# Moving small work between engines in the attention stage of a two-block transformer kernel: one head of a pair scaled on ScalarE, narrow top-k rounds paired, a log polynomial and six logarithms rearranged

## The chip, the cores and the metric

The kernel runs on one core of one Trainium2 chip. The metric is device time in microseconds (us), the median over repeated executions. All arithmetic of the reference is float32. The engines are named as in the profile: PE (TensorE, matrix products; PEld is its weight load), DVE (VectorE), ACT (ScalarE), POOL (GpSimd) and SP (SyncE, which issues the DMA transfers).

## The reference, cut to what matters

Two residual blocks of two layers each, on 256 tokens of width 1024. The change touches only the second block: its three attention branches.

```python
def _layer(x, positions, g_mix, w_in, b_forget, w_branch, w_out, g_mlp, w_up, w_down):
    h = _rmsnorm(x, g_mix)
    (qa, ka, va, qb, kb, vb, fl, qc, kc, vc, qi, ki, wi, gl) = split(h @ w_in)
    br_a = _stick_breaking_attention(qa, ka, va)              # 8 heads of 64
    log_f = log_sigmoid(fl + b_forget)                        # 256 x 8
    br_b = _forgetting_attention(qb, kb, vb, log_f)           # bias: cumsum of log_f
    br_c = _indexed_sparse_attention(rope(qc), rope(kc), vc, rope(qi), rope(ki), wi, top_k)
    gates = sigmoid(gl)
    x = x + (sum over branches of gates * (br @ w_branch)) @ w_out
    return x + square(relu(rmsnorm(x) @ w_up)) @ w_down

# stick breaking, per query row:
#   w = exp(log_sigmoid(z) + (sum of log_sigmoid(-z) over later keys)), strict causal mask
# forgetting: softmax(z + c[t] - c[s]) with c = cumsum(log_f)
# indexed sparse: score = sum_i w_i relu(q_i . k); keep the top_k = 64 keys; softmax over them
```

## The kernel before

A float32 product is made on PE as three products of rounded parts (`mm3`: high by high, high by low, low by high). So every float32 tile that PE multiplies is first *split*: a high part by a copy on ACT (L265 for weights, L297 for activations) and a low part by a subtraction on DVE (L267 and L298, for some weights POOL). Weights come from HBM in units of 512 KB, issued on SP some units ahead, and are split about three units before PE uses them. PE therefore carries a nearly unbroken stream of projections.

The attention branches are written as Python generators (`spawn`), each of which hands over at every `yield`. While the projections of the layer are written out, a tick after a group of matmuls lets two tasks of the deque take one step each. So a `yield` is not a wait on the chip: it sets how far apart two steps of a branch stand in the instruction streams of the engines, and what of the other branches and of the projections stands between them. Each engine runs its own stream in order; a wait for another engine's result holds up all that stands behind it on that engine. `wait(n)` is n yields, that is n turns.

The steps of one layer that the change touches:

- `neg_log1p_exp` (L887 to L906) computes log sigmoid for the forgetting branch's 256 x 8 gate inputs (tile 128x16): s = e/(2+e) with e = exp(-|x|), q = s*s, and a polynomial in q by Horner's rule, nine turns of a product (L901) and an addition of a constant (L902), each on the result of the one before. After it the result is multiplied by s (L904) and put together (L906). `lf_task` then copies it (L1624), and PE sums it up over the tokens by a product with a triangle of ones (L1630, L1631). The first block calls the same function.
- `dsa_task` (L1640 on), the sparse branch: index scores, then for each of the two blocks of 128 query rows eight rounds of `max` (L1667, the eight largest of a row) and `match_replace` (L1668), 64 keys in all. Rows of block 0 have 128 keys (narrow), rows of block 1 have 256. Then four pairs of heads, each with two calls of `attend`.
- `fox_task`, the forgetting branch: four pairs with two calls of `attend` each. It begins after `lf_task`.
- `attend` (L1462 on): scores on PE; on DVE scores plus mask or bias with the row maximum (L1471); the exponential with the row sum on ACT; the reciprocal of two sums (L1478) and the scaling of both heads on DVE (L1480); transposes on PE (L1485); the transposed heads copied out of PSUM, head 0 on DVE, head 1 on ACT (L1489). There are 32 calls in all: two branches, four pairs, two blocks, two layers.
- `sb_task`, the stick-breaking branch, six tiles of 128x512: log(1+exp) by ACT's Exp (L1773) and Ln (L1780), masks (DVE L1788, POOL L1790), then a split whose high part (L1796) and low part (L1798) are both made on POOL; PE sums the parts (L1802, L1803).

The order of the six splits is tiles 4, 5, 0, 1, 2, 3, and that of the six logarithms 0 to 5, with a turn after every second one. `after` lets a task begin when others are done. The order of instructions on each engine follows from these turns alone; there is no table of priorities.

Of the kernel before, what the change touches and what calls it, by code (L numbers as in the profile page):

```python
# [11 lines left out]
F32 = mybir.dt.float32  # L12
# [3 lines left out]
AF = mybir.ActivationFunctionType  # L16
ALU = mybir.AluOpType
# [83 lines left out]
def two_block_kernel(ctx: ExitStack, tc: tile.TileContext, A, out):  # L101
    nc = tc.nc
    pe, dve, act, pool, sp = nc.tensor, nc.vector, nc.scalar, nc.gpsimd, nc.sync

    def wait(n):
        for _ in range(n):
            yield
# [8 lines left out]
    tp = ctx.enter_context(tc.tile_pool(name="tp", bufs=2))  # L116
# [767 lines left out]
        for l in range(DEPTH):  # L884
            dve.tensor_scalar(nlam[:, l:l + 1], lam[:, l:l + 1], LAM_INIT[l], -1.0, op0=ALU.add, op1=ALU.mult)

    def neg_log1p_exp(o, x, n, pool_):  # L887

        e = T(pool_, [P, n], "lp_e")
        a = T(pool_, [P, n], "lp_a")  # L890
        s = T(pool_, [P, n], "lp_s")
        q = T(pool_, [P, n], "lp_q")
        dve.scalar_tensor_tensor(a, x, -1.0, x, op0=ALU.mult, op1=ALU.max)
        act.activation(e, a, AF.Exp, scale=-1.0)
        dve.tensor_scalar(a, e, 2.0, None, op0=ALU.add)
        dve.reciprocal(a, a)
        dve.tensor_tensor(s, e, a, op=ALU.mult)
        dve.tensor_tensor(q, s, s, op=ALU.mult)
        dve.memset(e, 1.0 / 19)
        for k in range(8, -1, -1):  # L900
            dve.tensor_tensor(e, e, q, op=ALU.mult)  # L901
            dve.tensor_scalar(e, e, 1.0 / (2 * k + 1), None, op0=ALU.add)  # L902
            yield
        dve.tensor_tensor(e, e, s, op=ALU.mult)  # L904
        dve.tensor_scalar(a, x, 0.0, None, op0=ALU.min)
        dve.scalar_tensor_tensor(o, e, -2.0, a, op0=ALU.mult, op1=ALU.add)  # L906
# [535 lines left out]
    xb = [xb[0], xb[1]]  # L1442


    SHE, SLE = pool, pool
    tri = cp.tile([P, 2, P], F32R, name="tri")
    dve.tensor_copy(tri[:, 0], C("negge"))
    dve.tensor_copy(tri[:, 1], C("negone"))
# [13 lines left out]
    def attend(tb, pair, scores, bias, v, pT):  # L1462

        S_ = P * (tb + 1)
        ps = sm_bank()[:, :2 * S_].rearrange("p (j s) -> p j s", j=2)
        scores(ps, tb, pair, S_)
        yield
        z = t2([P, 2, 256])[:, :, :S_]
        st = small(8)
        for j in range(2):  # L1470
            dve.tensor_tensor_reduce(z[:, j], ps[:, j], bias(tb, 2 * pair + j), 1.0, -3.0e38,  # L1471
                                     op0=ALU.add, op1=ALU.max, accum_out=st[:, j:j + 1])
        dve.tensor_scalar(st[:, 2:4], st[:, 0:2], -1.0, None, op0=ALU.mult)
        yield
        for j in range(2):
            act.activation(z[:, j], z[:, j], AF.Exp, bias=st[:, 2 + j:3 + j], accum_out=st[:, 4 + j:5 + j])
        yield
        dve.reciprocal(st[:, 6:8], st[:, 4:6])  # L1478
        for j in range(2):
            dve.tensor_scalar(z[:, j], z[:, j], st[:, 6 + j:7 + j], None, op0=ALU.mult)  # L1480
        yield
        pt = sm_bank()[:, :2 * S_].rearrange("p (j s) -> p j s", j=2)
        for j in range(2):
            for sb in range(tb + 1):
                pe.transpose(pt[:, j, sb * P:(sb + 1) * P], z[:, j, sb * P:(sb + 1) * P], ident)  # L1485
        yield
        for j in range(2):
            o = pT[j][:, 0:P] if tb == 0 else pT[j][:, P:3 * P]
            (act.copy if j else dve.tensor_copy)(o, pt[:, j])  # L1489
# [11 lines left out]
    def block2_layer(l, hT, rms):  # L1501
# [85 lines left out]
        lfx = T(tp, [P, 2, 8], "lfx")  # L1587
        lf = T(tp, [P, 2, 8], "lf")
# [27 lines left out]
        def lf_task():  # L1616
            yield from after([t_ki])

            f2 = lambda t: t.rearrange("p a b -> p (a b)")
            yield from neg_log1p_exp(f2(lf), f2(lfx), 16, tp)  # L1620
            lf2 = T(tp, [P, 2, 40], "lf2")
            pool.memset(lf2, 0.0)
            for k in range(2):
                dve.tensor_copy(lf2[:, :, 32 * k:32 * k + 8], lf)  # L1624

            nlo = cst[:, COFF["negle"][0]:COFF["negle"][0] + 256]
            for _ in range(LFY):
                yield
            ps = sm_bank()[0:40, 0:256]
            pe.matmul(ps, lf2[:, 0], nlo, start=True, stop=False)  # L1630
            pe.matmul(ps[:, P:], lf2[:, 1], nlo[:, :P], start=False, stop=True)  # L1631
            yield
            par = C("par")
            for k in range(2):
                act.activation(cs[0:40, k], ps, AF.Copy, scale=par[0:40, k:k + 1])
            for k in range(2):
                dve.scalar_tensor_tensor(cs[32:40, k], ps[32:40], par[32:40, k:k + 1], cs[32:40, k].bitcast(F32),
                                         op0=ALU.mult, op1=ALU.subtract)
# [4 lines left out]
        def dsa_task():  # L1643
            yield from after(t_c + [t_ki])
            for tb in range(2):
                S_ = P * (tb + 1)
                wv = small(4)
                dve.tensor_scalar(wv, tail[tb][:, 96:100], 0.5, None, op0=ALU.mult)
                scv = t2([P, 256])[:, :S_]
                for p_ in range(2):  # L1650
                    ps = sm_bank()[:, :2 * S_].rearrange("p (j s) -> p j s", j=2)
                    mm3(ps, *(t[:, p_, tb * P:(tb + 1) * P] for t in qiT), kiD[:, 0, :, :S_], kiD[:, 1, :, :S_],
                        start=True, stop=True)
                    yield
                    r = t2([P, 2, 256])[:, :, :S_]
                    act.activation(r, ps, AF.Relu, scale=0.125)
                    for j in range(2):
                        i = 2 * p_ + j
                        if i == 0:
                            dve.tensor_scalar(scv, r[:, j], wv[:, 0:1], None, op0=ALU.mult)  # L1660
                        else:
                            dve.scalar_tensor_tensor(scv, r[:, j], wv[:, i:i + 1], scv, op0=ALU.mult, op1=ALU.add)
                    yield
                dve.tensor_tensor(scv[:, tb * P:], scv[:, tb * P:], causal, op=ALU.add)
                m8 = small(8)
                for it in range(8):
                    dve.max(m8, scv)  # L1667
                    dve.match_replace(scv, m8, scv, GONE)  # L1668
                    yield
                M = Ms[tb]  # L1670
                dve.tensor_scalar(M, scv, -2.0e38, -NEG, op0=ALU.is_lt, op1=ALU.mult)
                dve.tensor_scalar(M, M, NEG, None, op0=ALU.add)
                dve.tensor_tensor(M[:, tb * P:], M[:, tb * P:], causal, op=ALU.add)
                yield

            def scores(ps, tb, pair, S_):
                qh, ql = (t[:, pair % 2, tb * P:(tb + 1) * P] for t in qcT[pair // 2])
                kh, kl = (t[:, pair // 2, :, :S_] for t in kbdC)
                mm3(ps, qh, ql, kh, kl, start=True, stop=True)

            branch(2)
            for pair in range(4):
                pT = [t2([P, 384]) for _ in range(2)]
                for tb in range(2):
                    yield from attend(tb, pair, scores, lambda tb_, h: Ms[tb_], None, pT)
                yield
                yield from attend_out(pair, pT, lambda sb, h: vc[sb][:, (h // 4) * 64:(h // 4 + 1) * 64], brT[2])
# [62 lines left out]
        def sb_task():  # L1750

            zs, ss = [], []
            for i in range(6):
# [11 lines left out]
                z = t2([P, 512])  # L1765
# [12 lines left out]
            dve.tensor_scalar(one, ss[5][:, 0:1], 0.0, 1.0, op0=ALU.mult, op1=ALU.add)  # L1778
            for i in range(6):
                act.activation(ss[i], ss[i], AF.Ln, bias=one)  # L1780
                dve.scalar_tensor_tensor(ss[i], zs[i], 0.0, ss[i], op0=ALU.max, op1=ALU.add)

                def diag(t):
                    if i < 4:
                        return t.rearrange("p (a b) -> p a b", a=2)[:, :, 0:P], 2
                    return t.rearrange("p (a b) -> p a b", a=4), 4
                d, n = diag(ss[i])
                dve.tensor_tensor(d, d, C("lt")[:, None, :].to_broadcast([P, n, P]), op=ALU.mult)  # L1788
                d, n = diag(zs[i])
                pool.tensor_tensor(d, d, C("ltneg")[:, None, :].to_broadcast([P, n, P]), op=ALU.add)  # L1790
                if i % 2:
                    yield
            sh, sl = {}, {}
            for i in (4, 5, 0, 1, 2, 3):
                sh[i] = t2([P, 512], F32R)
                SHE.tensor_copy(sh[i], ss[i])  # L1796
                sl[i] = t2([P, 512], F32R)
                SLE.tensor_tensor(sl[i], ss[i], sh[i].bitcast(F32), op=ALU.subtract)  # L1798
                yield
            for i in (4, 5, 0, 1, 2, 3):  # L1800
                ps = sm_bank()
# [204 lines left out]
```

## Time and profile before

| | |
|---|---|
| median of three runs | 1836.45 us (1836.09 to 1837.05) |
| profiled execution | 1836.55 us |
| its span, first to last instruction | 1834.7 us |
| PE busy | 1805.2 us (98%) |
| DVE, ACT, POOL busy | 1227.9 (67%), 906.8 (49%), 193.2 (11%) us |
| granted clock of PE, mean | 0.998 |

Block two begins at about 915 us. Its two layers run the same program, the second about 450 us after the first; the stage with the three branches lies between about 945 and 1120 us in the first.

How to read it: the span is cut into what each engine did. An idle stretch of PE is put down to the engine whose result ended it; idle time of an engine that is not the last to be waited for costs nothing. Instructions on DVE are pipelined, so the sum of their durations is a little more than the time from start to start.

### The profile page before, as it was taken

The numbers are of one execution on the slowest core, as the hardware profiler recorded it, in microseconds if no ns is written. First come the engines' busy times: TensorE is split into PE (matmuls) and PEld (weight loads), VectorE is DVE, ScalarE is ACT, GpSimd is POOL, SyncE is SP. The second block draws the span as 40 slices with busy tenths as digits, with TensorE's granted clock in tenths as the row PEclk, the third lists the DMA queues.
The fourth block names the chain that finished last, engine by engine and source line by source line (L and its number), as shares of the span: only waits on it lengthen the run. The fifth ranks groups of instructions, "written<-read, shape, count | busy, mean of one in ns | idle before, by whom it ended". The sixth has DMA issues, their size and how long they took to land.

```text
span 1834.7 us, 25022 instructions
## 1 busy us (share of the span) xinstructions
PE 1805.2 (98%) x9256; PEld 1487.3 (81%) x9256; DVE 1227.9 (67%) x2474; ACT 906.8 (49%) x1613; POOL 193.2 (11%) x131
## 2 busy tenths in 40 slices
PE   8999999999999999999999999999999999999998
PEld 4888888887888988878888777878888877788886
DVE  4754546566794935477879887565567978655665
ACT  4623333345343533465464684455566568444553
POOL 2020000001100101001020024010002003320000
PEclk9999999999999999999999999999999999999999
DMA  8533323233471432445744345445554435555552
GB/s 312 194 126 115 98 68 135 92 104 104 149 241 58 166 95 78 149 141 191 266 148 140 125 162 174 155 165 195 184 184 160 139 118 180 170 165 170 184 189 98
DMA packets 83611, 279.30 MB, mean 152 GB/s; under 512 B 13856, under 2 KB 14240, under 8 KB 83360
## 3 DMA queue, kind: packets, MB, share of 16 engines
q1 hardware_dynamic: 83488, 277.70, 45.2%
q8 instruction: 73, 1.20, 0.3%
q14 instruction: 50, 0.41, 0.1%
HBM read 276.61 MB, written 1.05 MB: 151 GB/s over the span
## 4 chain that ended last, share of the span: by engine, by line
PE 71%; DVE 8%; ACT 3%; issue 2%; POOL 2%; DMA 1%; DVEq 0%; POOLq 0%; ACTq 0%
PE mm L290 18%; PE mm L291 18%; PE mm L292 18%; PE sm L436 6%; DVE k L267 3%; PE sm L437 3%; PE sm L497 1%; ACT k L265 1%; PE sm L1243 1%; PE sm L1216 1%; DMA k<-in_w_modT 1%; PE sm L1496 1%; POOL k L1798 1%; PE sm L290 1%; PE sm L1485 1%
## 5 line engine op out<-in xcount | busy, mean ns | idle before, releaser
L290 PE MATMUL mm<-k,k 128*128 128x512 f32 (+1 forms) x2192 | 835.0, 381 | 3.1 <-ACT k L521 2.2
L291 PE MATMUL mm<-k,k 128*128 128x512 f32 (+1 forms) x2192 | 822.6, 375 | 0.0
L292 PE MATMUL mm<-k,k 128*128 128x512 f32 (+1 forms) x2192 | 821.9, 375 | 0.3 <-DVE k L523 0.3
L267 DVE TENSOR_TENSOR k<-k,k 128x1024 fp32r<-128x1024 f32 x441 | 552.8, 1271 | 173.6 <-ACT k L265 114.1
L265 ACT ACTIVATE k<-k 128x1024 fp32r<-128x1024 f32 x458 | 473.5, 1056 | 317.3 <-DVE k L267 138.9
L290 PEld LDWEIGHTS mm<-k,k 128*128 128x128 f32 x2192 | 413.3, 189 | 79.3 <-issue 6.0
L292 PEld LDWEIGHTS mm<-k,k 128*128 128x128 f32 x2192 | 413.3, 189 | 76.1 <-DVE k L523 1.3
L291 PEld LDWEIGHTS mm<-k,k 128*128 128x128 f32 x2192 | 413.8, 189 | 67.1 <-issue 0.5
L436 PE MATMUL sm<-k,k 128*128 128x512 f32 x448 | 158.9, 399 | 0.0
L437 PE MATMUL sm<-k,k 128*128 128x256 f32 x448 | 125.8, 281 | 0.0
L436 PEld LDWEIGHTS sm<-k,k 128*128 128x128 f32 x448 | 84.2, 188 | 20.7
L1872 DVE TENSOR_TENSOR k<-sm,k 128x256 f32<-128x256 f32 x56 | 22.6, 422 | 108.2 <-ACT k L1871 108.2
L1871 ACT ACTIVATE k<-sm 128x256 f32<-128x256 f32 x56 | 21.5, 384 | 130.8 <-PE sm L437 130.8
L437 PEld LDWEIGHTS sm<-k,k 128*128 128x128 f32 x448 | 84.6, 189 | 0.5
L707 DVE CUSTOM_DVE_ANT_0 k<-k,k 128x1024 f32<-128x1024 f32 x56 | 68.8, 1233 | 22.8 <-PE mm L291 20.3
L267 POOL TENSOR_TENSOR k<-k,k 128x1024 fp32r<-128x1024 f32 x17 | 43.3, 2571 | 336.9 <-DVE k L1839 171.7
L968 POOL TENSOR_TENSOR k<-k,k 128x512 f32<-128x512 f32 x16 | 23.4, 1470 | 287.2 <-DVE k L966 286.4
L298 DVE TENSOR_TENSOR k<-sm,k 128x256 fp32r<-128x256 f32 (+2 forms) x78 | 31.8, 413 | 32.5 <-ACT k L297 31.7
L297 ACT ACTIVATE k<-sm 128x256 fp32r<-128x256 f32 (+2 forms) x78 | 28.7, 374 | 45.6 <-PE sm L497 17.7
L483 ACT ACTIVATE k<-k 128x512 f32<-128x512 f32 x36 | 22.6, 628 | 47.6 <-DVE k L1839 20.2
L974 ACT ACTIVATE k<-mm 128x512 f32<-128x512 f32 x30 | 17.8, 596 | 54.1 <-PE mm L292 54.0
L1222 ACT ACTIVATE k<-sm,small 128x512 f32<-128x512 f32 (+1 forms) x48 | 29.1, 614 | 24.4 <-DVE small L1220 23.8
(299 smaller groups left out, 1705.1 us busy)
## 6 DMA issues: line engine op xcount, KB each, us to landing
k<-in_w_in SPq DMA_DIRECT2D x248, 512.0 KB, 3.5
k<-in_w_up SPq DMA_DIRECT2D x64, 512.0 KB, 4.2
k<-in_w_down SPq DMA_DIRECT2D x64, 512.0 KB, 3.9
k<-in_w_bo SPq DMA_DIRECT2D x48, 512.0 KB, 3.5
k<-in_w_modT SPq DMA_DIRECT2D x32, 512.0 KB, 3.5
k<-in_w_out SPq DMA_DIRECT2D x32, 512.0 KB, 4.2
k<-in_w_mod SPq DMA_DIRECT2D x16, 512.0 KB, 7.9
k<-in_c_rows SPq DMA_DIRECT2D x5, 512.0 KB, 3.6
```

The costliest lines, as they stand in the source:

```text
L265: act.activation(h, r, AF.Copy)
L267: (pool if i in slow else eng).tensor_tensor(lo, r, h.bitcast(F32), op=ALU.subtract)
L290: pe.matmul(ps, lh, rh, start=start, stop=False)
L291: pe.matmul(ps, lh, rl, start=False, stop=False)
L292: pe.matmul(ps, ll, rh, start=False, stop=stop)
L297: act.activation(h, src, AF.Copy)
L298: dve.tensor_tensor(lo, src, h.bitcast(F32), op=ALU.subtract)
L436: pe.matmul(ps[q], wh[:, k, s], acts.both(kt), start=(kt == 0), stop=False)
L437: pe.matmul(ps[q][:, :256], wl[:, k, s], acts.high(kt), start=False, stop=(kt == 2 * nk - 1))
L707: dve.tensor_tensor_reduce(o, w, sb[s], 0.5, 0.0, op0=ALU.mult, op1=ALU.add, accum_out=res[:, s, i - 1:i])
L968: pool.tensor_tensor(o, o, tt, op=ALU.add)
L1222: act.activation(e, ps[m], AF.Exp, scale=0.125, bias=st[:, 2 + m:3 + m], accum_out=st[:, 4 + m:5 + m])
```

## The change

Five edits, all in block two (`neg_log1p_exp` takes the engine as an argument and keeps DVE for block one):

1. The eighteen polynomial steps L901 and L902 are issued on POOL; L904 and L906 stay on DVE.
2. Of the two heads that `attend` scales, head 0 stays on DVE and head 1 is scaled by an ACT copy with a scale per row. The single turn behind it becomes `wait(1 + tb)`: two turns for block 1.
3. In block 0's top-k, the eight rounds take four turns, two rounds in each; block 1 is unchanged.
4. The six Ln are written without a turn between them; the DVE and POOL steps that follow each stand in a loop of their own, with the turns.
5. The high part of the stick-breaking split is copied by ACT; POOL keeps the subtraction.

```diff
-    def neg_log1p_exp(o, x, n, pool_):
+    def neg_log1p_exp(o, x, n, pool_, eng=dve):
...
         for k in range(8, -1, -1):
-            dve.tensor_tensor(e, e, q, op=ALU.mult)
-            dve.tensor_scalar(e, e, 1.0 / (2 * k + 1), None, op0=ALU.add)
+            eng.tensor_tensor(e, e, q, op=ALU.mult)
+            eng.tensor_scalar(e, e, 1.0 / (2 * k + 1), None, op0=ALU.add)
             yield
...
-    SHE, SLE = pool, pool
...
         dve.reciprocal(st[:, 6:8], st[:, 4:6])
-        for j in range(2):
-            dve.tensor_scalar(z[:, j], z[:, j], st[:, 6 + j:7 + j], None, op0=ALU.mult)
-        yield
+        dve.tensor_scalar(z[:, 0], z[:, 0], st[:, 6:7], None, op0=ALU.mult)
+        act.activation(z[:, 1], z[:, 1], AF.Copy, scale=st[:, 7:8])
+        yield from wait(1 + tb)
...
-            yield from neg_log1p_exp(f2(lf), f2(lfx), 16, tp)
+            yield from neg_log1p_exp(f2(lf), f2(lfx), 16, tp, pool)
...
                 for it in range(8):
                     dve.max(m8, scv)
                     dve.match_replace(scv, m8, scv, GONE)
-                    yield
+                    if tb or it % 2:
+                        yield
...
             for i in range(6):
                 act.activation(ss[i], ss[i], AF.Ln, bias=one)
+            for i in range(6):
                 dve.scalar_tensor_tensor(ss[i], zs[i], 0.0, ss[i], op0=ALU.max, op1=ALU.add)
...
-                SHE.tensor_copy(sh[i], ss[i])
+                act.activation(sh[i], ss[i], AF.Copy)
                 sl[i] = t2([P, 512], F32R)
-                SLE.tensor_tensor(sl[i], ss[i], sh[i].bitcast(F32), op=ALU.subtract)
+                pool.tensor_tensor(sl[i], ss[i], sh[i].bitcast(F32), op=ALU.subtract)
                 yield
```

Behind the removed line with `SHE`, the changed kernel's line numbers are lower by one (L1480 is L1478 and L1479 there), and from the loop of the six logarithms on higher by one.

DVE, first layer, around the polynomial, before (`lp_e`, `lp_q`, `lp_s`: the polynomial's sum, its argument q, and s; the rows of L267 and L298 are splits for projections):

```order
L905 TENSOR_SCALAR lp_a_8581<-lfx_8420 128x16
L901 TENSOR_TENSOR lp_e_8580<-lp_e_8580,lp_q_8583 128x16
L902 TENSOR_SCALAR lp_e_8580<-lp_e_8580 128x16
L267 TENSOR_TENSOR k_1781_8713<-k_1754_8544,k_1780_8712 128x1024
L298 TENSOR_TENSOR k_1669_8169<-sm_8562,k_1669_8169 64x128
L1509 SCALAR_TENSOR_TENSOR k_1768_8618<-mm_8443,k_1705_8312 128x512
L298 TENSOR_TENSOR k_1669_8169<-sm_8562,k_1669_8169 64x128
L901 TENSOR_TENSOR lp_e_8580<-lp_e_8580,lp_q_8583 128x16
L902 TENSOR_SCALAR lp_e_8580<-lp_e_8580 128x16
L901 TENSOR_TENSOR lp_e_8580<-lp_e_8580,lp_q_8583 128x16
L298 TENSOR_TENSOR k_1727_8426<-k_1768_8618,k_1726_8425 128x512
```

And the same place in the changed kernel:

```order
L905 TENSOR_SCALAR lp_a_8581<-lfx_8420 128x16
L267 TENSOR_TENSOR k_1781_8722<-k_1754_8544,k_1780_8721 128x1024
L298 TENSOR_TENSOR k_1669_8169<-sm_8562,k_1669_8169 64x128
L1508 SCALAR_TENSOR_TENSOR k_1768_8618<-mm_8443,k_1705_8312 128x512
L298 TENSOR_TENSOR k_1669_8169<-sm_8562,k_1669_8169 64x128
L904 TENSOR_TENSOR lp_e_8580<-lp_e_8580,lp_s_8582 128x16
L906 SCALAR_TENSOR_TENSOR lf_8421<-lp_e_8580,lp_a_8581 128x16
L1623 COPY lf_1782_8740<-lf_8421 128x2x8 x2
L298 TENSOR_TENSOR k_1727_8426<-k_1768_8618,k_1726_8425 128x512
```

The product with s (L904), which needs POOL's last polynomial step, now stands behind L905 with four instructions between; before, it stood 34 rows further down, between two top-k rounds.

PE, first layer, around the first transposes of `attend` (tile `sm_...<-cst` is the transpose with the identity; `mm_...` are projections), before:

```order
L290 MATMUL mm_9019<-k_1638_8023,k_1847_9050 128x256
L291 MATMUL mm_9019<-k_1639_8024,k_1847_9050 128x256
L292 MATMUL mm_9019<-k_1638_8023,k_1848_9051 128x256
L1485 MATMUL sm_9011<-cst,k_1821_8955 128x128
L290 MATMUL sm_9034<-k_1670_8171,k_1697_8286 128x512
L1485 MATMUL sm_9011<-cst,k_1821_8955 128x128
```

And in the changed kernel, ten rows earlier in PE's stream:

```order
L290 MATMUL mm_9035<-k_1638_8023,k_1848_9060 128x256
L291 MATMUL mm_9035<-k_1639_8024,k_1848_9060 128x256
L292 MATMUL mm_9035<-k_1638_8023,k_1849_9061 128x256
L1484 MATMUL sm_8951<-cst,k_1814_8917 128x128
L290 MATMUL sm_8970<-k_1670_8171,k_1697_8286 128x512
L291 MATMUL sm_8970<-k_1671_8173,k_1697_8286 128x512
L292 MATMUL sm_8970<-k_1670_8171,k_1698_8287 128x512
L290 MATMUL sm_9022<-k_1730_8429,k_1726_8425 128x256
L291 MATMUL sm_9022<-k_1731_8431,k_1726_8425 128x256
L1484 MATMUL sm_8951<-cst,k_1814_8917 128x128
```

The transpose of head 0 comes ten 256-column matmuls earlier, and scores of two further calls of `attend` now stand between it and the transpose of head 1.

ACT, first layer, around the six logarithms (L1410 is the exponential of another stage, L1811 that of the stick-breaking weights; `ACT_TABLE_LOAD` changes the function table), before:

```order
L1780 ACT_TABLE_LOAD
L1780 ACTIVATE k_1971_9714<-k_1971_9714,small_9963 128x512
...
L1780 ACTIVATE k_2002_9853<-k_2002_9853,small_9963 128x512
L1410 ACT_TABLE_LOAD
L1410 ACTIVATE k_2023_9961<-mm_9878,rms_7855 128x512
L1410 ACTIVATE k_2025_9979<-mm_9889,rms_7855 128x512
L1780 ACT_TABLE_LOAD
L1780 ACTIVATE k_2009_9886<-k_2009_9886,small_9963 128x512
L1780 ACTIVATE k_2016_9916<-k_2016_9916,small_9963 128x512
...
L1811 ACT_TABLE_LOAD
```

And in the changed kernel:

```order
L1780 ACT_TABLE_LOAD
L1780 ACTIVATE k_1969_9701<-k_1969_9701,small_9963 128x512
...
L1780 ACTIVATE k_2008_9877<-k_2008_9877,small_9963 128x512
L1410 ACT_TABLE_LOAD
L1410 ACTIVATE k_2023_9961<-mm_9864,rms_7855 128x512
L1780 ACT_TABLE_LOAD
L1780 ACTIVATE k_2016_9914<-k_2016_9914,small_9963 128x512
L1410 ACT_TABLE_LOAD
L1410 ACTIVATE k_2025_9983<-mm_9880,rms_7855 128x512
L1797 ACTIVATE k_2031_10017<-k_2008_9877 128x512
```

Four logarithms and then two have become five and then one; the sixth stands between the two exponentials of L1410.

## Rows read from the trace of the kernel before

**Rows 1.** The page, part 1: busy time of each engine.

```profile
PE 1805.2 (98%) x9256; PEld 1487.3 (81%) x9256; DVE 1227.9 (67%) x2474; ACT 906.8 (49%) x1613; POOL 193.2 (11%) x131
```

**Rows 2.** PE's waits; columns: line, releaser, us in total, times, longest us.

```profile
PE sm L1803 <- POOL k L1798: 2.5, 4, 1.0
PE sm L1485 <- DVE k L1480: 2.1, 2, 1.1
PE sm L1630 <- DVE lf L1624: 0.8, 1, 0.8
PE sm L1630 <- issue: 0.8, 1, 0.8
```

**Rows 3.** Windows: length; busy PE, PEld, DVE, ACT, POOL (instructions); clock, DMA share, GB/s.

```profile
966.00:977.00 11.00, 10.94 (x89) 10.60 (x87) 10.67 (x39) 5.61 (x9) 0.00 (x0) 1.00 0.43 144
984.60:1006.00 21.40, 20.50 (x136) 18.62 (x134) 20.68 (x56) 9.80 (x18) 3.77 (x4) 1.00 0.37 125
```

**Rows 4.** PE timeline, first layer; columns: start us, us, instruction, idle before.

```profile
977.70 0.60 PE L1630 MATMUL sm<-cst,lf 128*40 128x256 f32 x2 [0.76 <-issue]
...
1002.66 0.28 PE L292 MATMUL mm<-k,k 128*128 128x256 f32 x1
...
1006.18 0.33 PE L1485 MATMUL sm<-cst,k 128*128 128x128 f32 x1 [1.08 <-DVE k L1480]
...
1100.02 0.39 PE L1803 MATMUL sm<-k,tri 128*128 128x512 f32 x1
...
1104.32 0.50 PE L1803 MATMUL sm<-k,tri 128*128 128x512 f32 x1 [0.96 <-POOL k L1798]
```

**Rows 5.** DVE timeline, first layer, polynomial to first scaling.

```profile
963.88 0.18 DVE L901 TENSOR_TENSOR lp_e<-lp_e,lp_q 128x16 f32<-128x16 f32 x1
964.09 0.17 DVE L902 TENSOR_SCALAR lp_e<-lp_e 128x16 f32<-128x16 f32 x1
964.20 1.23 DVE L267 TENSOR_TENSOR k<-k,k 128x1024 fp32r<-128x1024 f32 x1
...
966.70 0.18 DVE L901 TENSOR_TENSOR lp_e<-lp_e,lp_q 128x16 f32<-128x16 f32 x1
...
976.64 0.17 DVE L904 TENSOR_TENSOR lp_e<-lp_e,lp_s 128x16 f32<-128x16 f32 x1
...
1005.84 0.48 DVE L1480 TENSOR_SCALAR k<-k,small 128x128 f32<-128x128 f32 x2
```

**Rows 6.** DVE timeline, first layer: a weight split whose unit PE takes up at 1002.66.

```profile
997.65 1.22 DVE L267 TENSOR_TENSOR k<-k,k 128x1024 fp32r<-128x1024 f32 x1
```

**Rows 7.** POOL by source line, whole span: ns min/median/max, first and last start.

```profile
L1622 POOL MEMSET lf<- x2: 164/164/164, 0.7 to 0.8; 128x80 f32 x2
L968 POOL TENSOR_TENSOR k<-k,k x16: 1272/1293/2274, 126.1 to 767.5; 128x512 f32<-128x512 f32 x16
L267 POOL TENSOR_TENSOR k<-k,k x17: 2351/2408/3411, 16.7 to 1649.3; 128x1024 fp32r<-128x1024 f32 x17
```

**Rows 8.** POOL timeline, first layer, stick-breaking splits.

```profile
1095.65 0.94 POOL L1796 CAST k<-k 128x512 fp32r<-128x512 f32 x1 [0.69 <-DVE k L1788]
...
1104.21 1.60 POOL L1796 CAST k<-k 128x512 fp32r<-128x512 f32 x1
1105.89 2.15 POOL L1798 TENSOR_TENSOR k<-k,k 128x512 fp32r<-128x512 f32 x1
...
1111.77 0.61 POOL L1796 CAST k<-k 128x512 fp32r<-128x512 f32 x1
1112.46 1.30 POOL L1798 TENSOR_TENSOR k<-k,k 128x512 fp32r<-128x512 f32 x1
```

**Rows 9.** DVE's L267 by source, 1096 to 1119 us, beside POOL's work.

```profile
L267 DVE TENSOR_TENSOR k<-k,k x10: 1207/1698/2310, 1097.2 to 1118.9; 128x1024 fp32r<-128x1024 f32 x10
```

**Rows 10.** ACT: the copies of L1489 by source (whole span), a table load of the timeline.

```profile
L1489 ACT COPY k<-sm x32: 240/309/393, 1007.5 to 1525.0; 128x128 f32<-128x128 f32 x16, 128x256 f32<-128x256 f32 x16
1088.40 1.28 ACT L1410 ACT_TABLE_LOAD   x1
```

## Prediction

> **What bounds the kernel now.** I read the busy line first: PE is busy 1805.2 of 1834.7 us [rows 1]. A change to the other engines can then win only what PE idles, and must be read from PE's waits. Second, these waits: of those that the change touches, the transposes of attention on DVE's scaled heads cost 2.1 us in two layers, the cumulative sum L1630 1.6 (in one layer put down to the copy before it, in the other to "issue"), the stick-breaking sums L1803 on POOL's subtraction 2.5 [rows 2]; 6.2 us of 1834.7 in all, and the most that a perfect version could win there. Third, the windows say who is behind these waits: between 966 and 977, and between 984.6 and the first transposes, DVE works 10.67 of 11.00 and 20.68 of 21.40 us, POOL 0 and 3.77 [rows 3]. So in this stretch DVE is the engine whose order sets when the first attention weights are ready, and PE comes just 1.08 us too early [rows 4]. Whatever lifts work from DVE there pays up to 1.08 us per layer; whatever makes DVE wait there costs the full length, less that lift.
>
> The profiled execution took 1836.55 us, 1.85 more than its span, against a median of 1836.45; the sum is made against the former and 0.1 is taken off. I call 0.2%, 3.7 us, what a measurement of this kernel can tell from no change.
>
> **Edit 1, the polynomial on POOL.** DVE loses 18 instructions. The first pair took from 963.88 to 964.20, 0.32 us [rows 5]; later ones lie close to it, so by 0.15 an instruction 2.7 us leave DVE per layer, 0.32 of them ahead of the first L267. But order now has L904, which needs POOL's last step, only four instructions behind. Those four ended before 966.70 [rows 5], so DVE is at L904 at 966.70 - 0.32 = 966.4. From there nothing on DVE passes: weight splits, top-k rounds, and the row maxima of attention stand behind it.
>
> When is POOL done? No row shows a 16-column two-input step or an addition of a constant on POOL. From 1293 ns at 512 columns and 2408 at 1024 [rows 7] a two-input step costs 2.18 ns a column and 0.18 us fixed, so 16 columns come to 0.21. For the one-input step I take 0.18: 0.61 for 512 columns [rows 8] and 0.164 for a memset of 80 [rows 7]. A step on the result of the one before starts 0.08 behind its end (1111.77 + 0.61 to 1112.46) [rows 8]. Nine pairs of 0.21 + 0.18 + 2 x 0.08 = 0.55 make 4.95 us. POOL is idle then; DVE is not: beside DVE's L267 the same copy took 1.60 in place of 0.61 [rows 8]. One L267 of 1.23 lies beside the chain before DVE stops, so 1.0 is added: 5.95. POOL starts at 963.9 to 964.0, ends near 969.9, and DVE stands 969.9 - 966.4 = 3.5 us.
>
> The bounds. Below: at the 0.15 of DVE per step without any gap, 2.7 us, no wait at L904 to speak of (966.7 against 966.4). Above: if each step cost the 0.61 of a 512-column copy plus 0.08, 12.4 us, a stall of 10. I take 3.5, near the fit, as both its ends are measured without DVE beside them.
>
> [...]
>
> **From the stall to PE.** In the old order DVE took from 966.70 (the place of the new L904) to the first scaled head at 1005.84 + 0.28, 39.4 us. Of it the other polynomial steps go, 2.4, and 0.4 for two row maxima that now come later; 0.3 I give back for lost overlap: 36.9. With the stall the head is ready at 969.9 + 36.9 = 1006.8. PE was there at 1006.18 - 1.08 = 1005.10 [rows 4]; it now has ten 256-column matmuls fewer ahead, at 11.0 / 89 = 0.123 us [rows 3] 1.2, and no 0.76 before L1630: 1003.1. It waits 3.7 + 0.06 = 3.8 in place of 1.08: **+2.7 per layer**. Next late are weight splits: L267 at 997.65 ended at 998.87 [rows 6], PE took that unit at 1002.66 [rows 4], 3.8 us to spare. DVE is later by 3.5 - 2.4 = 1.1 and PE earlier by 0.8; 1.9 is left, so nothing.
>
> L1630: lf is ready about 970.5 in place of 977.5, PE comes near 977: **-0.78 per layer**. Gone only if the chain takes over 11 us.
>
> **Edits 2 and 3, one head on ACT, paired rounds.** DVE loses a scaling (0.28 to 0.35) in each of 32 calls; ACT gains one, by its nearest rows 0.24 to 0.39 [rows 10]. Head 0 was the last before PE's first transpose already, so the first wait loses nothing by this. ACT is busy 9.80 of 21.40 us there [rows 3]; a copy that finds a weight copy ahead comes up to 1.06 us later, for which the second turn and the matmuls between the two transposes are cover. Cost 0 to +0.5 per layer, taken **+0.2**. The paired rounds are what moved PE's place, counted above.
>
> **Edits 4 and 5, logarithms and the high parts.** Order shows four table loads before and four after, of 1.28 us on ACT [rows 10]; ACT is not waited for there, so 0. POOL loses the copies. It needed 1.61 + 2.15 plus gaps = 3.8 us for one tile; PE's next sum, its wait taken off, stood 1104.32 - 0.96 - 1100.02 = 3.3 after the one before [rows 4, 8]. With 2.15 + 0.08 POOL keeps ahead, and PE's waits of L1803 go, 2.5 in two layers [rows 2]: **-1.25 per layer**. ACT's copies are long done by then.
>
> **Sum.** +2.7 - 0.78 + 0.2 - 1.25 = +0.87 per layer, +1.7 in two: 1838.2 against the profiled execution, **1838.1 us**. No change that can be told.
>
> **Rivals.** *A, the chain is hidden.* POOL's steps follow each other at DVE's pace, 2.7 us. Then the head is ready at 966.7 + 36.9 = 1003.6, PE waits 0.5 in place of 1.08: -0.6 - 0.78 + 0.2 - 1.25 = -2.4 a layer, 1831.6. For it: a memset of 80 columns costs 0.164 [rows 7], no more than DVE's own steps. Against it: each step reads what the one before wrote, and the one such pair that rows 8 show has a gap. Chance 0.2.
>
> *B, the chain is longer: slower.* At 0.44 a step, gap included (halfway between the fit's 0.28 and the copy's 0.61), it takes 7.9, with an L267 beside it 8.9; the stall is 6.5, the wait 6.8: +5.7 - 0.78 + 0.2 - 1.25 = +3.9 a layer, and the split of [rows 6] is about 1 us late at most: 1844.2. It decides from a chain of 6.9 us on, where two layers reach +3.7. For it: L1798 took 2.15 beside DVE against 1.30 [rows 8]. Against it: the fit. Chance 0.27.
>
> *C, ACT's place in the line.* Head 1 now waits on ACT behind a weight copy, in both branches, after DVE's reciprocal. If three of a layer's sixteen calls make PE wait one such copy of 1.06, +3.2 a layer: 1844.5. For it: head 1's product and the copies of L1489 stand in one queue. Against it: PE has matmuls of other calls between. Chance 0.06.
>
> *D, first use.* An addition of a constant has not run on POOL before; if its first use held POOL, the first layer alone would stall that much more: 1841 if it held it for 3 us. The first cast in the trace took 0.94 with DVE as its releaser [rows 8], where 0.61 to 1.60 is usual, so no such hold is seen. Chance 0.02. [...]
>
> Edit 4 not doing what its name says is not a rival with a time of its own: four table loads stay either way.
>
> **How the numbers follow.** Forecast 0.45, A 0.2, B 0.27, C and D 0.08. The forecast's own range, with the chain from 4.6 to 6.9, is 1835.5 to 1840. The range for 8 in 10 takes in A's 1831.6 and most of B: 1831 to 1844.5. Faster by over 0.2%: A, 0.2. Slower: B, C, D and 0.01 of the forecast, 0.36. Within: 0.44.
>
> **What would show it.** In the changed kernel's trace: 18 POOL rows of 128x16 in about 6 us from 964; an idle stretch of 3 to 4 us on DVE ahead of L904, released by POOL; a wait of 3 to 4 us at the first L1484, twice; no wait at L1629 and L1804; DVE rows back to back in between. The forecast is wrong if DVE's wait is under 1 us or over 5, or if L1484 waits in many calls.

## The result and the profile after

The changed kernel takes 1853.96 us (median of five runs, 1852.75 to 1854.57) against 1836.45, 17.5 us slower; the ratio, taken from the means of the executions as all ratios here, is 1.0093 [1.0079, 1.0108]. (One of ten executions of x3_log_cast below took 2382 us at a mean clock of 0.70 and is left out of its ratio.) The forecast was 1838.1 with a range up to 1844.5. The profiled execution took 1854.19 us; at the start of block two it was already 1.7 us behind that of before. That arose in its first 30 us, ahead of all that the change touches, so some 16 us belong to the change.

The page's first part of the changed kernel:

```profile
PE 1812.8 (98%) x9255; PEld 1494.1 (81%) x9256; DVE 1220.5 (66%) x2406; ACT 924.1 (50%) x1657; POOL 190.0 (10%) x155
```

Against [rows 1], PE is busy 7.6 us *longer* on the same matmuls (one record is missing). Its waits (line, releaser, us in total, times, longest):

```profile
PE sm L1484 <- DVE k L1478: 10.2, 4, 4.8
PE mm L290 <- DVE k L1508: 3.1, 2, 1.5
...
PE sm L1495 <- DVE k L1488: 1.9, 2, 0.9
```

Against [rows 2]: L1630 and L1803 are gone, the transposes have risen from 2.1 to 10.2, two new waits have come. The first place, on PE's timeline of the first layer (start, us, instruction, idle before):

```profile
1004.52 0.28 PE L291 MATMUL mm<-k,k 128*128 128x256 f32 x1
1004.64 0.28 PE L292 MATMUL mm<-k,k 128*128 128x256 f32 x1
1009.69 0.48 PE L1484 MATMUL sm<-cst,k 128*128 128x128 f32 x1 [4.76 <-DVE k L1478]
...
1013.33 0.42 PE L292 MATMUL mm<-k,k 128*128 128x256 f32 x1
1013.54 0.42 PE L290 MATMUL mm<-k,k 128*128 128x256 f32 x1
...
1014.98 0.28 PE L291 MATMUL mm<-k,k 128*128 128x256 f32 x1
1015.10 0.28 PE L292 MATMUL mm<-k,k 128*128 128x256 f32 x1
```

The same matmul starts every 0.12 us ahead of the wait, every 0.21 behind it, and every 0.12 again from 1014 on. The windows give the reason in their granted clock (the number after the five engines' busy times):

```profile
1004.00:1005.00 1.00, 0.92 (x8) 0.72 (x6) 0.93 (x4) 0.14 (x1) 0.00 (x0) 1.00 0.89 225
...
1008.00:1009.00 1.00, 0.00 (x0) 0.00 (x0) 1.00 (x3) 1.00 (x5) 0.00 (x0) 0.50 0.00 0
...
1013.00:1014.00 1.00, 1.00 (x6) 1.00 (x7) 0.59 (x7) 0.88 (x4) 0.00 (x0) 0.50 0.00 0
1014.00:1015.00 1.00, 1.00 (x10) 1.00 (x10) 0.36 (x1) 0.52 (x3) 0.00 (x0) 0.96 0.03 8
```

During the wait the granted clock falls from 1.00 to 0.50 and comes back 4.4 us after PE has taken up work. In the second layer the same wait (4.76 us) is followed by 6.6 us of PE's work at 0.50, and a later place by 3.4 us more. Before, no such window between 940 and 1700 us was below 1.00. (In the expectations below, 1.2 GHz stands for this granted clock of 0.50; as an estimate from these rows, 256 columns in 0.21 us are 1.2 columns per ns.)

The polynomial on POOL and DVE beside it, first layer:

```profile
965.62 0.22 POOL L901 TENSOR_TENSOR lp_e<-lp_e,lp_q 128x16 f32<-128x16 f32 x1 [19.29 <-DVE lp_a L905]
965.94 1.11 POOL L902 TENSOR_SCALAR lp_e<-lp_e 128x16 f32<-128x16 f32 x1
967.13 0.22 POOL L901 TENSOR_TENSOR lp_e<-lp_e,lp_q 128x16 f32<-128x16 f32 x1
967.45 0.25 POOL L902 TENSOR_SCALAR lp_e<-lp_e 128x16 f32<-128x16 f32 x1
967.78 0.22 POOL L901 TENSOR_TENSOR lp_e<-lp_e,lp_q 128x16 f32<-128x16 f32 x1
...
971.97 0.25 POOL L902 TENSOR_SCALAR lp_e<-lp_e 128x16 f32<-128x16 f32 x1
```

```profile
965.70 1.23 DVE L267 TENSOR_TENSOR k<-k,k 128x1024 fp32r<-128x1024 f32 x1
...
972.25 0.17 DVE L904 TENSOR_TENSOR lp_e<-lp_e,lp_s 128x16 f32<-128x16 f32 x1 [4.09 <-POOL lp_e L902]
...
1009.35 0.29 DVE L1478 TENSOR_SCALAR k<-k,small 128x128 f32<-128x128 f32 x1
```

A pair of steps takes 0.65 us, and the chain 6.6. The one step beside DVE's L267 took 1.11 in place of 0.25 and ended 0.12 behind it. DVE stands 4.09 us at L904, and what stands behind it waits with it: the next split, L298, starts only at 972.83.

The second place is near 1050 us, where before PE had no wait. PE, then DVE:

```profile
1051.43 0.62 PE L1495 MATMUL sm<-k,k 128*64 128x256 f32 x2 [0.94 <-DVE k L1488]
...
1053.74 0.38 PE L1718 MATMUL sm<-k,pairs 40*128 40x256 f32 x1
1055.66 0.50 PE L290 MATMUL mm<-k,k 128*128 128x512 f32 x1 [1.54 <-DVE k L1508]
```

```profile
1054.16 0.29 DVE L1470 CUSTOM_DVE_ANT_0 k<-sm,cst 128x128 f32<-128x128 f32 x1 [1.98 <-PE sm L1718]
...
1054.91 0.69 DVE L1508 SCALAR_TENSOR_TENSOR k<-mm,k 128x512 f32<-128x512 f32 x1
```

Steps of both attention branches stand so close here that PE and DVE wait for each other in turn: PE for the copied heads, DVE's row maximum (L1470) for PE's scores (L1718), and PE's next projection for L1508, which stands behind that row maximum in DVE's stream though it needs none of it.

**Where the 16 us are.** PE's rows of the two executions, two layers together: first transposes 9.52 - 2.14 = +7.4; L1630 -1.6; L1803 -2.6; the place near 1050 (0.31 + 0.94 + 1.54, and two short ones at 1029 and 1077, 2.98 a layer) +6.0. That is +9.2. What is left, 6.8, is the slow clock: 4.4 + 6.6 + 3.4 = 14.4 us of PE's work at a clock of 0.50 lose 7.2, by an estimate of half of them.

### The profile page after: what moved, and what is told of

Read it like the earlier page. It is cut to its first block, busy times and chain, and to the rows that moved or that the text cites. A ratio compares the mean times of both kernels' runs of the same rounds, so it can differ in the third digit from the quotient of the medians.

```text
span 1852.4 us, 25024 instructions
## 1 busy us (share of the span) xinstructions
PE 1812.8 (98%) x9255; PEld 1494.1 (81%) x9256; DVE 1220.5 (66%) x2406; ACT 924.1 (50%) x1657; POOL 190.0 (10%) x155
## 5 line engine op out<-in xcount | busy, mean ns | idle before, releaser
L267 DVE TENSOR_TENSOR k<-k,k 128x1024 fp32r<-128x1024 f32 x441 | 554.1, 1274 | 178.3 <-ACT k L265 107.8
L267 POOL TENSOR_TENSOR k<-k,k 128x1024 fp32r<-128x1024 f32 x17 | 43.3, 2567 | 337.2 <-DVE k L1840 171.7
L298 DVE TENSOR_TENSOR k<-sm,k 128x256 fp32r<-128x256 f32 (+2 forms) x78 | 31.9, 414 | 30.6 <-ACT k L297 29.9
```

The source lines that it names most:

```text
L267: (pool if i in slow else eng).tensor_tensor(lo, r, h.bitcast(F32), op=ALU.subtract)
L298: dve.tensor_tensor(lo, src, h.bitcast(F32), op=ALU.subtract)
```

## The experiments

All ratios are to the kernel before, run beside each.

**Which edits.** Four kernels: the changed one with edit 1 undone (the diff below); and the kernel before with edit 1 alone, with edits 4 and 5 alone, and with edits 2 and 3 alone, each as in the diff ahead of the prediction.

```diff
-            yield from neg_log1p_exp(f2(lf), f2(lfx), 16, tp, pool)
+            yield from neg_log1p_exp(f2(lf), f2(lfx), 16, tp)
```

> The changed kernel with edit 1 undone (polynomial back on DVE). Theory S (three parts: DVE's stall at the polynomial makes the long wait at the first transposes; that wait is followed by a stretch at 1.2 GHz; and edits 2 and 3 put steps of the two attention branches side by side, 2.8 us of waits per layer around 1050 us): first transposes wait 2 to 2.5 us per layer instead of 4.76, no stretch at 1.2 GHz behind them, the waits around 1050 stay, the wait before L1629 is back (0.8). Time about 1843 us, +6 to +7 over before. Rival R (the turns of edits 2 and 3 alone bring PE too early to the transposes; the polynomial hardly matters): wait over 4 us and the 1.2 GHz stretch stay, 1852 us or more.

> The kernel before with edit 1 alone (polynomial on POOL). [...] Rival R: same as before within 1 us. A third view, that the polynomial on POOL is the whole loss: 1850 or more.

> The kernel before with edits 4 and 5 alone (six logarithms written together, high parts copied by ACT). Theory S and rival R both: the waits of the stick-breaking sums on POOL go, -1.25 us per layer, 1834 us; the first transposes wait 1.08 as before. If ACT's copies come late instead: the same waits, now on ACT, and no gain.

> The kernel before with edits 2 and 3 alone (head 1 scaled on ACT, an added turn for the second block, narrow top-k rounds paired). Theory S: first transposes wait 2 to 2.5 us, waits of 2.8 us per layer around 1050, L1803's waits as before or gone by the shift; +4 us per layer, about 1845. Rival R: 4.76 us and the 1.2 GHz stretch also here, 1852 or more.

Measured: 1845.51 (1.0044 [1.0029, 1.0059]), 1846.15 (1.0047 [1.0032, 1.0062]), 1833.03 (0.9978 [0.9968, 0.9988]) and 1847.28 us (1.0054 [1.0039, 1.0069]). So edit 1 costs 8 to 9 us, whether alone or beside the others (the prediction's terms for it, +2.7 - 0.78 a layer, come to 3.8), edits 2 and 3 together 10, and edits 4 and 5 gain 4; rival R falls, and the polynomial is not the whole loss. With the polynomial on DVE the first wait is 1.90 and, in the second layer, 1.84, a little under what was expected; with edit 1 alone it is 4.54:

```profile
1004.94 0.33 PE L1484 MATMUL sm<-cst,k 128*128 128x128 f32 x1 [1.90 <-DVE k L1478]
```

```profile
1009.58 0.48 PE L1485 MATMUL sm<-cst,k 128*128 128x128 f32 x1 [4.54 <-DVE k L1480]
```

The first of these rows is x1_poly_on_dve, the second x2_poly_only. In the latter the wait is the old 1.08, the stall of 4.09 and the 0.76 that PE no longer spends ahead of L1630, less 1.4: of the 2.7 us lifted from DVE only half came back. The waits account for 5.4 us of the loss; 11.3 us of PE's work at a clock of 0.50 (1008 to 1015 and 1465 to 1472) cost, by an estimate of half of them, about as much again. In x1_poly_on_dve and x4_heads_pairs the waits near 1050 are those of the changed kernel, with a clock of 0.50 behind them in both layers. Against what was expected, 0.50 also follows the first transposes of their second layer, behind a wait of 1.84 and 1.85.

In x3_log_cast PE's waits of L1803 are gone. They were 2.6 us of idle time, yet each of the two layers became 2.1 us shorter, 4.2 in all. The kernel before shows why:

```profile
1102.96 0.39 PE L1802 MATMUL sm<-k,tri 128*128 128x512 f32 x1
1104.32 0.50 PE L1803 MATMUL sm<-k,tri 128*128 128x512 f32 x1 [0.96 <-POOL k L1798]
1104.65 0.39 PE L290 MATMUL mm<-k,k 128*128 128x512 f32 x1
```

Matmuls overlap: these otherwise start every 0.23 us, though a row lasts 0.39. Here the starts are 1.36 and 0.33 apart, so 0.96 of idle time cost 1.23. Three such waits a layer cost 2.15, which is all that edits 4 and 5 gain.

**Edits 2 and 3 apart, and the idle time filled.** The first two kernels are that before with one edit of the diff; the third is x2_poly_only with this, ahead of the first transposes of each layer (`fill[0]` is set once in each):

```diff
+        if fill[0]:
+            fill[0] = 0
+            for _ in range(36):
+                pe.matmul(pt.rearrange("p j s -> p (j s)")[:, :256], tri[:, 0], tri.rearrange("p j s -> p (j s)"),
+                          start=True, stop=True)
         for j in range(2):
             for sb in range(tb + 1):
                 pe.transpose(pt[:, j, sb * P:(sb + 1) * P], z[:, j, sb * P:(sb + 1) * P], ident)
```

> The kernel before with edit 2 alone (head 1 scaled on ACT, an added turn for the second block). Edits 2 and 3 together cost 10 us: 0.8 us per layer at the first transposes, 2.8 at about 1045 to 1049 us, and stretches at 1.2 GHz behind both. View T (the added turn brings the two branches side by side): the 2.8 us are here too, about 1842. View U (neither edit does it alone): first transposes wait 1.1 us as before, no wait near 1049, 1836 to 1838.

> The kernel before with edit 3 alone (narrow top-k rounds paired). PE is at the first transposes 1.2 us earlier in its stream and DVE is not faster, so that wait is about 2.3 in place of 1.08: 1839 to 1840. View T: no waits near 1049. View P (the pairing brings the branches side by side): 2.8 us per layer there too, and a stretch at 1.2 GHz behind it, 1845.

> Edit 1 alone as in x2_poly_only (1846.2 us), with 36 extra matmuls of 256 columns put before the first transposes of each layer, whose results nothing uses: they take 36 x 0.12 = 4.3 us, about the 4.53 us that PE stands idle there. Theory S (an idle stretch of this length is what is followed by 1.2 GHz): clock 1.0 throughout, wait under 0.5 us, and the time falls by the 5.6 us that the two slow stretches cost, to 1840.5, though PE has more to do. If the slow clock has another cause: it stays, and the time is 1846 or more.

Edit 2 alone: 1854.72 (1.0095 [1.0081, 1.0109]), as slow as all five edits together and far from both views. It has no wait near 1049, but one at a place that nobody named, the stick-breaking sums. PE, then POOL, DVE and ACT ahead of it:

```profile
1107.95 0.50 PE L1802 MATMUL sm<-k,tri 128*128 128x512 f32 x1 [2.40 <-POOL k L1796]
...
1110.15 0.80 PE L1803 MATMUL sm<-k,tri 128*128 128x512 f32 x1 [1.47 <-POOL k L1798]
...
1111.17 0.63 PE L291 MATMUL mm<-k,k 128*128 128x512 f32 x1
```

```profile
1097.13 0.81 POOL L1790 TENSOR_TENSOR k<-k,cst 128x256 f32<-128x256 f32 x1 [3.22 <-DVE k L1781]
1096.29 0.69 DVE L1781 SCALAR_TENSOR_TENSOR k<-k,k 128x512 f32<-128x512 f32 x1 [2.89 <-ACT k L1780]
1094.24 1.28 ACT L1780 ACT_TABLE_LOAD   x1
```

POOL makes the high parts late because its masks wait for DVE's L1781, which waits for the logarithms on ACT. Edit 2 has spread these among the exponentials of L1410: ACT loads a function table six times there, where before it did so four times. PE's last row takes 0.63 where the same form takes 0.40 at a clock of 1.00: the windows from 1109 to 1115 show 0.50 once more. Waits and clock make up some 11 of the 17 us that this kernel loses; the rest was not traced. With edit 3 beside it (x4_heads_pairs) this place has no such wait and four table loads, so the edits do not add up one by one.

Edit 3 alone: 1841.44 (1.0027 [1.0018, 1.0037]), its first waits 1.88 and 1.84, smaller ones of 0.77 and 0.43 near 1065, the clock 1.00 in every window from 940 to 1700 us. Neither kernel has the waits near 1050; that much of view U holds.

x8_filler took 1849.51 (1.0072 [1.0058, 1.0085]) and did not test the theory: its matmuls ran at 995 us, and the wait of 4.6 was still there, with a clock of 0.50 behind it. This shows that the order does not follow from the turns alone, as the part ahead of the prediction has it: when the program is built, an instruction is moved up to where it can run (two transposes written together had other matmuls between them in the order of before, too).

**The turn, and DVE without a wait for POOL.** The first part of the diff is y1 (with the polynomial on DVE), the rest y2 (the changed kernel), all of it y3:

```diff
-        yield from wait(1 + tb)
+        yield from wait(1)
...
-        dve.tensor_tensor(e, e, s, op=ALU.mult)
+        eng.tensor_tensor(e, e, s, op=ALU.mult)
...
-        dve.scalar_tensor_tensor(o, e, -2.0, a, op0=ALU.mult, op1=ALU.add)
+        if eng is dve:
+            dve.scalar_tensor_tensor(o, e, -2.0, a, op0=ALU.mult, op1=ALU.add)
+        else:
+            eng.tensor_scalar(e, e, -2.0, None, op0=ALU.mult)
+            eng.tensor_tensor(o, e, a, op=ALU.add)
...
-                dve.tensor_copy(lf2[:, :, 32 * k:32 * k + 8], lf)
+                pool.tensor_copy(lf2[:, :, 32 * k:32 * k + 8], lf)
```

> The changed kernel with the polynomial on DVE (as x1_poly_on_dve, 1845.5 us) and with one turn behind the scaling in both blocks in place of wait(1 + tb). View T (the added turn, together with the paired rounds, puts the two branches side by side): the waits of 2.9 us per layer near 1042 to 1049 us and the stretches at 1.2 GHz behind them go, the first transposes still wait 1.9 us: 1836 us. View P (paired rounds and head 1 on ACT do it without the turn): those waits stay, 1845.

> The changed kernel with all that follows the polynomial (L904, L906, the two copies) on POOL too, so that DVE never waits for POOL there. Theory S: the first transposes wait about 2.2 us (1.9 of x1_poly_on_dve, 0.56 since L1629 waits no more, less 0.3) in place of 4.76, the waits near 1050 and the slow clock behind them stay: 1844 to 1846 against 1854. Rival (the polynomial on POOL costs through something other than DVE's wait at L904): 4.8 us and 1854 stay.

> y2_after_all_pool with one turn in place of wait(1 + tb). View T: 2.2 us at the first transposes and no other wait, 1834 to 1837. View P: as y2_after_all_pool, 1844 to 1846.

y1: 1844.80 (1.0046 [1.0031, 1.0060]), with waits of 0.30, 0.76 and 1.21 us between 1042 and 1048 and new ones of 0.31 and 0.90 near 1068: the added turn is not the cause, view T falls. Paired rounds and head 1 on ACT bring the waits about together; neither does alone, and why the two meet only then was not settled. y2: 1845.81 (1.0046 [1.0031, 1.0061]), first wait 2.15, against 4.76 with DVE waiting for POOL. So moving four more instructions to POOL takes back 8 us of edit 1: it was DVE's wait at L904 that cost, not POOL's steps. y3: 1846.22 (1.0047 [1.0030, 1.0064]), like y2.

**What pays.** Edits 4 and 5 with the whole log on POOL, as in y2, and that with edit 2's scaling and a single turn:

> The kernel before with edits 4 and 5, and with the polynomial and all behind it (the product with s, the end of the log and the two copies for the cumulative sum) on POOL, so that no DVE instruction waits for POOL there. Theory S: DVE loses 3.3 us of work and never stands at L904, the first head is ready before PE comes; waits at L1630 (0.78) and at the first transposes (1.08) go in each layer: 1833.0 - 3.7 = 1829.3. Rival (the cost of edit 1 is POOL's steps beside DVE's splits, not the wait at L904): the first transposes still wait over 3 us, 1840 or more.

> x7_all_on_pool (1831.5 us) with head 1 scaled on ACT and one turn as before, rounds not paired. DVE loses 0.3 us in each of 32 calls, but the first head is scaled as before: the wait of 1.58 us at the first transposes stays. If edit 2 harms only by its added turn: 1830 to 1832. If a scaling on ACT in itself delays head 1 behind weight copies: waits at other transposes, 1835 or more.

1831.47 (0.9971 [0.9961, 0.9982]) and 1833.50 (0.9980 [0.9971, 0.9990]): faster than both kernels, and not told apart from x3_log_cast or from each other. The mechanism was half right. L1630 waits no more, but the first transposes do:

```profile
1007.10 0.33 PE L1489 MATMUL sm<-cst,k 128*128 128x128 f32 x1 [1.58 <-DVE k L1484]
```

1.58 against 1.08 + 0.78 = 1.86: PE gains 0.3. Yet the polynomial and what follows it had taken 3.1 us on DVE before, from start to start. DVE's waits in that stretch (964 to 1008 us; before, it had none ahead of the first scaling) show where half of it went:

```profile
DVE k L267 <- ACT k L265: 1.1, 2, 0.7
...
DVE k L298 <- ACT k L297: 0.4, 1, 0.4
```

Without the polynomial DVE comes early to splits that ACT has not yet copied, and waits 1.5 us for them; in the second layer it is 1.5 too. The rounds of top-k, each step of which needs the one before, take 12.9 us in place of 12.3. The other 0.7 is spread over small steps.

**The filler, placed.** The same 36 matmuls with an edge for the order alone, from each to the reciprocal ahead of the scaling:

```diff
-        dve.reciprocal(st[:, 6:8], st[:, 4:6])
+        rc = dve.reciprocal(st[:, 6:8], st[:, 4:6])
...
+                f = pe.matmul(pt.rearrange("p j s -> p (j s)")[:, :256], tri[:, 0], tri.rearrange("p j s -> p (j s)"),
+                              start=True, stop=True)
+                tc.add_manual_dep(f.ins, rc.ins.name, mybir.DependencyInfo(mybir.DependencyClass.NoSync, mybir.DependencyReason.DATA), reason="place")
```

> Edit 1 alone as in x2_poly_only (1846.2 us, PE idle 4.53 us ahead of the first transposes of each layer, 1.2 GHz for some 6 us behind them), with 36 extra matmuls of 256 columns, whose results nothing uses, now placed directly ahead of those transposes in PE's stream (in x8_filler they had come 10 us earlier and the idle stretch was still there). Theory S (the slow clock follows PE's idle stretch): the 36 take 4.3 us of it, about 0.6 us of waiting is left, clock 1.0 throughout, and the time falls by the 5.6 us lost at 1.2 GHz, to about 1840.5, though PE has 72 matmuls more to do. If the slow clock has another cause (DVE's stall, the transposes, ACT): it stays, 1846.

```profile
1002.01 4.48 PE L1488 MATMUL sm<-tri 128*128 128x256 f32 x36
1007.16 0.53 PE L1493 MATMUL sm<-cst,k 128*128 128x128 f32 x2 [0.67 <-DVE k L1482]
1009.24 0.44 PE L1493 MATMUL sm<-cst,k 128*128 128x128 f32 x2 [0.85 <-DVE k L1482]
```

```profile
1002.00:1007.00 5.00, 4.49 (x38) 4.29 (x36) 4.90 (x20) 3.23 (x8) 0.00 (x0) 1.00 0.17 68
1007.00:1015.00 8.00, 6.99 (x43) 5.47 (x44) 5.27 (x22) 5.04 (x16) 0.00 (x0) 1.00 0.19 66
```

Clock 1.00 throughout, in both layers, while DVE still stands 4.08 us at L904. In x8_filler the same matmuls stood earlier, and the idle stretch (4.6 us) and the clock of 0.50 stayed. So at this place it was PE's idle time that brought the slow clock.

The time is another matter: 1844.67 (1.0046 [1.0029, 1.0063]), not told from x2_poly_only, and not 1840.5. The filler and the wait behind it take 5.2 us where the idle stretch took 4.5. And the order behind it is not that of x2_poly_only: the transposes of the second call of `attend` start 2.1 us behind the first, and PE waits 0.85 for them. In x2_poly_only they start 6.1 us behind, without a wait:

```profile
1015.63 0.27 PE L1485 MATMUL sm<-cst,k 128*128 128x128 f32 x1
```

So this run shows what brought the slow clock at the first transposes, and leaves open how much time its absence gives back.

## Why the prediction was wrong, step by step

The prediction had the mechanism of edit 1: POOL's chain, DVE's stall, PE's wait. By its own signs of being wrong it would have stood, with a stall of 4.09 us, between 1 and 5, and waits in few calls. Two steps failed: it put the loss from edits 2 and 3 near nothing, and it had no term for PE's clock behind a wait.

- *POOL's chain, 5.95 us; stall, 3.5.* Measured 6.6 and 4.09. The fit from 512 and 1024 columns gave 0.21 and 0.18 for the steps; they took 0.22 and 0.25. The surcharge for one L267, 1.0, was 0.86. A size, 0.6 too small. The one-input step was sized by a cast (0.61 for 512 columns) and a memset, while POOL had run a one-input TENSOR_SCALAR, a product, at L754 from 19 us on, in 1.57 us or more for 512 columns; rival D left it out as well.
- *From L904 to the first head, 36.9 us.* 972.25 to 1009.64: 37.4. The wait was then forecast at 3.8 and is 4.76: the term +2.7 per layer measured +3.7.
- *L1630, -0.78, and L1803, -1.25 per layer.* Both waits went, -0.8 and -1.3 of idle time. In time L1803 is worth 2.1, as x3_log_cast shows, so the 6.2 us of waits were not "the most that a perfect version could win": these waits cost more than their idle time.
- *Edits 2 and 3, "0 to +0.5 per layer, taken +0.2".* This step failed. The place near 1050 costs 3.0 a layer in waits, and x4_heads_pairs shows that edits 2 and 3 bring it. The sum moved PE's place at the first transposes and looked no further along the stream, though the order showed scores of two more calls between two transposes. Rival C, at 0.06, looked at later calls, but for waits on ACT; the three waits here end on DVE (L1478, L1488, L1508).
- *No term for the clock.* The largest failure: 6.8 of 16 us, and z1_filler_placed (1.00 where x2_poly_only has 0.50) shows that PE's idle time brought it at the first transposes. The reading "whatever makes DVE wait there costs the full length, less that lift" took a wait of PE for its length. Rival B's chain of 8.9 us did not come; and even with its wait of 6.8 us it gave only 1844.2, since it lacked this term too.
- *"Whatever lifts work from DVE there pays up to 1.08 us per layer"*, read from 20.68 of 21.40 us busy [rows 3]. x7_all_on_pool shows 0.3 of 3.1 us. A busy share of 97% was no proof that DVE's throughput alone set the end: with the polynomial gone, DVE waits 1.5 us for ACT's copies, and its dependent rounds take 0.6 longer.
- *Edit 4.* It was not run alone. In x3_log_cast the waits of L1803 explain the whole gain, so nothing is left for it there, as forecast. That "four table loads stay either way" holds for these kernels; other edits of the turns gave six (x5_heads_only) and two (x6_pairs_only, y1, y3).

In the end a layer's sum, the mean of the two, reads +3.7 - 0.8 - 1.3 + 3.0 + 3.4 = +8.0 where the prediction had +0.87.

## What to carry to other kernels

In this kernel, with PE 98% busy, the price of the new waits on PE was their length plus the slow clock that followed some of them: 9.2 us of waits brought 6.8 us more, so a plan that risks a wait of a few us in one place must win nearly twice that elsewhere. Before lending steps to a slower engine (here 0.65 us for a pair of steps on POOL against 0.32 on DVE), look where the first instruction that needs them stands in the lender's own stream: move it, and all up to the next engine, along with them. And of two edits that shift the turns of interleaved tasks, test each alone and together.

## What the runs showed of the hardware that was not expected

The length of a wait alone did not tell whether the slow clock, 0.50, followed. First transposes, by the length of the wait: 1.56 to 1.62 us (x7_all_on_pool, y4_best_heads), followed by it in none of four; 1.84 to 1.90 (x1, x4, x6, y1), in three of eight, always in the second layer; 2.15 (y2, y3), in all four; 4.5 to 4.8 (the changed kernel, x2, x8), in all six. The place near 1050 had 0.50 behind its last wait (1.2 to 1.5 us) in both layers of x1, x4, y2 and y3, in the first of y1 and in the second of the changed kernel. What decides is open. The stretches that followed covered 3.4 to 6.6 us of PE's work in the changed kernel.
